# Token halves of a seven-product FFN in equal chunks, operand sums on VectorE, staged fetch for the output stage

## The chip, the cores and the metric

One NeuronCore of a Trainium2 chip runs the whole program. The metric is device time of one execution in microseconds (us), as the median of the runs shown; lower is better. The profile is one execution of the same program, taken by the hardware profiler, with times from the span's start.

## What is computed

The reference is one inference step of a two-layer backbone over 128 prompt tokens and 1024 latent tokens (1152 in all, width 1024). Layer 0 mixes tokens by retention and pooling, layer 1 by attention. Each layer ends in a SwiGLU feed-forward block (FFN), which is where the change lies. Cut to that:

```python
D_MODEL = 1024
D_FF = -(-8 * D_MODEL // (3 * 256)) * 256          # 2816

def swiglu(h, w_in, w_out):
    a, b = jnp.split(h @ w_in, 2, axis=-1)
    return (jax.nn.silu(a) * b) @ w_out

for i in range(DEPTH):                             # 2 layers
    ...                                            # mixer, residual
    fs = swiglu(rmsnorm(xs, norm_gain[i, 2]) * (1.0 + sc2s) + sh2s, w_ffn_in[i], w_ffn_out[i])
    xs = xs + g2s * rmsnorm(fs, norm_gain[i, 3])
```

Prompt tokens (xp) go the same way with their own shift, scale and gate.

## The kernel before

All matrix products keep fp32 accuracy by splitting each operand into a rounded part (hi, type fp32r) and a remainder (lo), and by summing three matmuls, hi·hi + hi·lo + lo·hi. `split` (L155 to L157) makes the pair: ScalarE (ACT) casts hi at L156, VectorE (DVE) subtracts at L157. `mm3` (L174 to L179) issues the three matmuls.

**Input half of the FFN.** The hidden width is cut in 22 tiles of 128 (f). For one f the two weight blocks (128 columns of a and 128 of b, each in two halves of the model width) form a 2x2 block matrix, and the normalised tokens form another: two halves of the model width by two halves of 576 tokens. Their product is taken in Winograd's form, with 7 block products instead of 8: P1 to P7. `PROD` (L762) says for each which weight piece or weight sum it takes ("a" or "s" and a number), which token operand (0 to 6) and which of four PSUM regions. `product` (L829) issues one: two chunks of token columns, each with 4 steps of the model width times 3 matmuls, so 24 matmuls; before, the chunks have 192 and 384 columns (L836). `prep` (L817) splits the weights of a product into one of three slots. `sums` (L809) makes the four weight sums of the next f on GpSimd (POOL). `after` (L847) takes a finished product out of PSUM; at P3 the tile's result is written to DRAM (L872).

**Prologue.** The token operands 2 to 6 are sums of token blocks and must be made first. `first_half` (L886) transposes and splits the first 576 tokens. `second_half(j, b)` (L898), eight calls, transposes tokens 576 to 1151 for one j of four and one of two column ranges (b=0: 192 wide, b=1: 384 wide), and makes the operands: sums t1 to t4 and a cast (ACT) and a subtraction for each operand. Three of the subtractions (L915, L927, L928) are on GpSimd, the rest on DVE. While this goes on, the PE runs products that need only the first operands: P1 and P2 of the first `NPRO` = 4 tiles, 8 products (`pro`, L772). They use two PSUM regions in turn, because the transposes take the other half of PSUM. `run` (L930) puts the order: product s, then `second_half`, then `after(s)`, then `prep(s + 3)`.

**Output half.** `output` (L999) multiplies the 22 tiles by w_ffn_out: 9 token tiles x 2 halves of the width, in chunks of f tiles given by `NCH`; each chunk's partial sum goes to the buffer O, by an ACT copy in the first chunk (L1038) and a DVE add after that (L1040). 22 x 18 x 3 = 1188 matmuls of 512 columns. `out_prep(f)` (L989) fetches tile f and its weights from DRAM (L992, L994), and splits them; it is called for the first two tiles during the last f of the input half and then for the tiles of the next chunk. All tiles are fetched into the same staging buffer XGT[4096:5248].

**What sets the order.** The text is handed to a list scheduler, which gives each engine its fixed sequence by a model of readiness: an instruction may be issued ahead of earlier text if its inputs are expected sooner. On the chip every engine then runs its sequence strictly in order, so an instruction that waits holds all behind it. In layer 0 small units of the next layer's adaLN projection (`Ada.unit`, `hook`) are woven into the FFN; their work is on DVE (L345) and PE (L326).

Of the kernel before, what the change touches and what calls it, by code (L numbers as in the profile page):

```python
# [10 lines left out]
F32 = mybir.dt.float32  # L11
# [53 lines left out]
def hybrid_step_kernel(ctx: ExitStack, tc: tile.TileContext, a: dict, outs: list):  # L65
# [699 lines left out]
    class FFN:  # L765
# [3 lines left out]

        def __init__(self, l, mid1, xs, xd, next_sub):  # L770
            self.l, self.M1, self.xs, self.xd, self.next_sub = l, mid1, xs, xd, next_sub
            pro = [(0, P1), (1, P1), (0, P2), (1, P2), (2, P1), (3, P1), (2, P2), (3, P2)]  # L772
            self.steps = pro + [(f, p) for f in range(NF)
                                for p in ((P6, P7, P5, P4, P3) if f < NPRO else (P1, P6, P7, P5, P2, P4, P3))]
            self.npro = len(pro)
            self.wi = a["w_ffn_in"][l].rearrange("(k p) f -> p k f", p=128)


        def xop(self, i, k, lo, c0, w):
            o = (2 * k + lo) * 576 + c0  # L780
            if i == 5:
                return self.M1[:, o:o + w]
            if i == 6:
                if (k, lo) == (3, 1):
                    return self.M1[:, 4608:4800] if c0 == 0 else RR[:, 26112:26496]
# [7 lines left out]

        def pieces(self, f, pro):
            if pro:
                b = (RAW[:, 0], RAW[:, 1], O[:, 6:8, 0:512], RAW[:, 0])[f]
# [12 lines left out]
        def sums(self, f):  # L809
            a11, a12, a21, a22 = self.pieces(f, False)  # L810
            s = [O[:, 4 + i, 576:1088] for i in range(4)]
            nc.gpsimd.tensor_tensor(s[0], a21, a22, op=ALU.add)
            nc.gpsimd.tensor_tensor(s[1], s[0], a11, op=ALU.subtract)
            nc.gpsimd.tensor_tensor(s[2], a11, a21, op=ALU.subtract)
            nc.gpsimd.tensor_tensor(s[3], a12, s[1], op=ALU.subtract)
# [13 lines left out]
        def product(self, s):  # L829
            f, p = self.steps[s]  # L830
            _, _, x, reg = PROD[p]
            if s < self.npro:
                reg = 1 - f % 2
            wh, wl = self.slot(s)
            first = p not in (P2, P3, P4)
            for c0, w, o in ((0, 192, 320), (192, 384, 512)):  # L836
                ps = PS[:, 1024 * reg + o:1024 * reg + o + w]
                n = 0
                for k in range(4):
                    ks = slice(128 * k, 128 * k + 128)  # L840
                    xh, xl = self.xop(x, k, 0, c0, w), self.xop(x, k, 1, c0, w)
                    for u, v in ((wh, xh), (wh, xl), (wl, xh)):
                        nc.tensor.matmul(out=ps, lhsT=u[:, ks], rhs=v, start=first and n == 0, stop=n == 11,  # L843
                                         skip_group_check=not first)
                        n += 1

        def after(self, s):  # L847
            f, p = self.steps[s]
            reg = PROD[p][3] if s >= self.npro else 1 - f % 2
            ps = PS[:, 1024 * reg + 320:1024 * reg + 896]  # L850
            u2, u3, c22, s1, sl = (XGT[:, 576 * i:576 * i + 576] for i in range(5))
            if f < NPRO:
                s1, sl = O[:, 2 * f, 0:576], O[:, 2 * f + 1, 0:576]
            g1, g2 = XGT[:, 2880:3456], XGT[:, 3456:4032]
            if p == P1:
                nc.scalar.copy(s1, ps)  # L856
# [41 lines left out]
        def second_half(self, j, b):  # L898

            ts, c0, w, p0 = (((4, 5), 0, 192, 64), ((6, 7, 8), 192, 384, 0))[b]  # L900
            if b == 0:
                bufs = [XGT[:, 4096 + 192 * i:4288 + 192 * i] if j % 2 == 0 else O[:, 4 + i // 3, 192 * (i % 3):192 * (i % 3) + 192]
                        for i in range(6)]
            else:
                bufs = [XGT[:, 384 * i:384 * i + 384] for i in ((0, 1, 2, 3, 8, 9) if j % 2 == 0 else (4, 5, 6, 7, 8, 9))]
            x12, x22, t1, t2, t3, t4 = bufs
            for n, (k, tm) in enumerate(((j, x12), (j + 4, x22))):
                ps = bank(4 + 2 * (j % 2) + n)
# [2 lines left out]
                self.evac_h(k, ps[:, p0:p0 + w], tm, ((1, 0, w),))  # L911
            op = lambda i, lo: self.xop(i, j, lo, c0, w)
            nc.vector.tensor_sub(t1, x12, op(0, 0))
            nc.vector.tensor_sub(t1, t1, op(0, 1))
# [3 lines left out]
            nc.vector.tensor_sub(t2, x22, t1)  # L918
            nc.scalar.copy(op(3, 0), t2)
            nc.vector.tensor_sub(op(2, 1), t1, op(2, 0))  # L920
            nc.vector.tensor_sub(t4, op(1, 0), t2)  # L921
            nc.vector.tensor_add(t4, t4, op(1, 1))  # L922
            nc.scalar.copy(op(5, 0), t4)
            nc.scalar.copy(op(4, 0), t3)
            nc.vector.tensor_sub(op(3, 1), t2, op(3, 0))
            nc.vector.tensor_sub(op(5, 1), t4, op(5, 0))
            nc.gpsimd.tensor_tensor(op(6, 1), x22, op(6, 0), op=ALU.subtract)  # L927
            nc.gpsimd.tensor_tensor(op(4, 1), t3, op(4, 0), op=ALU.subtract)  # L928

        def run(self):  # L930
            l = self.l
# [3 lines left out]
            for s in range(len(self.steps)):  # L935
                f, p = self.steps[s]
                self.product(s)
                if s < self.npro:
                    if s < 2:
                        next(tail, None)  # L940
                    if s < 7:
                        self.second_half((s + 1) % 4, (s + 1) // 4)
                    self.after(s)
                    if s + 3 < self.npro:
                        self.prep(s + 3)
                    if s == 0:
                        self.load(2, True, (0, 1))
                    elif s == 1:
                        self.load(3, True, (0, 1))
                        self.load(0, False, (2, 3))  # L950
                    elif s == 5:
                        self.load(0, False, (0, 1))
                    elif s == 6:
                        self.sums(0)
                        self.load(1, False, range(4))
                        self.prep(8)
                        self.prep(9)
                    elif s == 7:
                        self.prep(10)
                    continue  # L960
                self.after(s)
                self.prep(s + 3)
# [3 lines left out]
                    adaq.extend([Ada(1, 0, bufs, 2, True), Ada(1, 1, bufs, 2, True)])  # L966
                if f >= NPRO and p in (P7, P5):
                    hook()
                if (f, p) == (NF - 1, P1):
                    self.out_prep(1)  # L970
                elif (f, p) == (NF - 1, P7):
                    self.out_prep(0)
            self.output()


        def out_slot(self, f):
            M1, M2 = self.M1, mid2r["t"]
            r = lambda o, w: RR[:, o:o + w]
            one = lambda b: (b[:, 0:1152], b[:, 1152:2304], [b[:, 2304:2816], b[:, 2816:3328]], [b[:, 3328:3840], b[:, 3840:4352]])
            i = f % 7  # L980
            if i in (0, 1, 2, 3):
                return one(r((13824, 18432, 4608, 0)[i], 4352))
            if i == 4:
                return one(M1[:, 0:4352])
            if i == 5:
                return M2[:, 0:1152], M2[:, 1152:2304], [M2[:, 2304:2816], M2[:, 2816:3328]], [r(12288, 512), r(12800, 512)]
            return r(22784, 1152), r(23936, 1152), [r(25088, 512), r(25600, 512)], [r(26112, 512), r(13312, 512)]

        def out_prep(self, f):  # L989
            gh, gl, wh, wl = self.out_slot(f)  # L990
            gr = XGT[:, 4096:5248]
            nc.sync.dma_start(out=gr, in_=gg_scr[self.l][f])  # L992
            w = raw()
            nc.sync.dma_start(out=w, in_=a["w_ffn_out"][self.l, f * 128:(f + 1) * 128, :])  # L994
            split(gh, gl, gr)
            for h in range(2):
                split(wh[h], wl[h], w[:, 512 * h:512 * h + 512])

        def output(self):  # L999
            l = self.l  # L1000
            last_layer = self.next_sub is None
            if l == 0:
                nc.gpsimd.memset(XGT[:, 2048:3072], 0.0)
                adaq.append(Ada(1, 2, ada_bufs(XGT[:, 0:4096]), 4))
# [375 lines left out]
```

## Time and profile before

| | |
|---|---|
| median of 3 runs | 3034.7 us (3032.24 to 3035.81) |
| profiled execution, own time | 3034.96 us |
| its span | 3032.7 us, granted TensorE clock 0.988 |
| first input-half product, layer 0 / layer 1 | 693.76 / 2172.23 us |
| first product that needs the second token half (P6 of tile 0), layer 0 / 1 | 749.12 / 2232.31 us |
| first matmul of the output half, layer 0 / 1 | 1265.9 / 2734.29 us |

The page gives busy time by engine. PE is the matmul engine and PEld its weight load. In rows of groups the figures behind the bar are busy us, mean ns of one instruction, then idle time of its engine ahead of them and what ended it ("<-ACT O L1038": an ACT instruction of line 1038 that works on O). In timeline rows the first two numbers are start and length in us; matmuls in a row overlap, so n of them with a spacing p take (n - 1) p plus the length of one.

### The profile page before, as it was taken

The page shows a single profiled execution, that of the slowest core. Times are in us where ns is not written, and L with a number is a line of the kernel's source. Part 1 is how long each engine was busy: PE and PEld are TensorE (multiplying, and loading weights), DVE is VectorE, ACT ScalarE, POOL GpSimd, SP SyncE. Part 2 cuts the span into 40 slices and gives each one's busy share as a digit, 9 for nine tenths or more (in the row PEclk, how much of TensorE's full clock was granted, in tenths as well). Part 3 has the DMA queues.
Part 4 walks back from the last instruction along what each step waited for, and adds up shares of the span by engine and source line. Part 5 has one row for each costly group of instructions (what it writes and reads, how often), then busy time and mean ns, then how long its engine had stood idle before and what let it go on. Part 6 is the DMA issues. An engine that isn't in the chain of part 4 may idle for free. (4 is left out here: it accounts for less than half of the span.)

```text
span 3032.7 us, 44867 instructions
## 1 busy us (share of the span) xinstructions
PE 2927.0 (97%) x17979; PEld 2640.9 (87%) x17979; DVE 1763.9 (58%) x2793; ACT 1047.3 (35%) x1950; POOL 581.1 (19%) x766
## 2 busy tenths in 40 slices
PE   7999999998999999899999999999989999998998
PEld 4889998787999999777779988888789999997886
DVE  5783347438656666546775567884674444443554
ACT  5222223325222222321243367773532222233211
POOL 2010012115322222100034521111252222210000
PEclk9999999999999999999999999999989999999999
DMA  7531111412433333424331000002222222224322
GB/s 240 171 100 48 34 41 35 137 59 70 131 95 106 111 98 96 134 100 138 123 137 49 22 15 1 29 29 84 84 69 83 66 77 70 69 79 138 104 81 97
DMA packets 191945, 261.54 MB, mean 86 GB/s; under 512 B 10157, under 2 KB 137577, under 8 KB 191609
## 3 DMA queue, kind: packets, MB, share of 16 engines
q1 hardware_dynamic: 180160, 216.83, 22.9%
q0 software_dynamic: 11088, 41.47, 3.5%
q8 instruction: 141, 2.31, 0.3%
q14 instruction: 68, 0.55, 0.1%
q10 hardware_dynamic: 488, 0.38, 0.0%
HBM read 212.47 MB, written 46.17 MB: 85 GB/s over the span
## 5 line engine op out<-in xcount | busy, mean ns | idle before, releaser
L179 PE MATMUL PS<-RR 128*128 128x256 f32 (+2 forms) x6000 | 1068.5, 332 | 22.8 <-ACT O L1038 21.8
L179 PEld LDWEIGHTS PS<-RR 128*128 128x128 f32 x6000 | 910.8, 191 | 129.8 <-ACT O L1038 23.0
L843 PE MATMUL PS<-RR 128*128 128x192 f32 (+1 forms) x5324 | 797.6, 309 | 30.8 <-ACT O L856 15.3
L843 PEld LDWEIGHTS PS<-RR 128*128 128x128 f32 x5324 | 775.1, 193 | 41.8 <-ACT O L856 17.2
L156 ACT CAST RR<-O 128x512 fp32r<-128x512 f32 (+1 forms) x242 | 151.8, 627 | 566.2 <-PE PS L843 415.7
L179 PE MATMUL PS<-RR,MID2True 128*128 128x512 f32 (+1 forms) x1524 | 312.0, 343 | 0.1
L156 ACT CAST RR<-RAW 128x512 fp32r<-128x512 f32 (+1 forms) x187 | 135.7, 738 | 397.6 <-PE PS L179 152.6
L179 PEld LDWEIGHTS PS<-RR,MID2True 128*128 128x128 f32 x1524 | 238.9, 189 | 35.1 <-ACT MID1False L711 0.5
L157 DVE TENSOR_TENSOR RR<-RAW,RR 128x512 fp32r<-128x512 f32 (+1 forms) x187 | 157.9, 857 | 148.8 <-ACT RR L156 125.6
L1040 DVE TENSOR_TENSOR O<-PS,O 128x512 f32<-128x512 f32 x216 | 147.9, 688 | 159.2 <-PE PS L179 158.0
L157 DVE TENSOR_TENSOR RR<-O,RR 128x512 fp32r<-128x512 f32 (+1 forms) x242 | 173.0, 715 | 63.4 <-ACT RR L156 63.1
L184 POOL TENSOR_SCALAR SM<-SM 128x1 f32<-128x1 f32 (+1 forms) x153 | 52.8, 345 | 791.2 <-ACT PS L220 306.1
L345 DVE SCALAR_TENSOR_TENSOR O<-O,PW 128x512 f32<-128x512 f32 x224 | 161.0, 765 | 24.8 <-DMA O<-in_w_ada_dram 13.7
L843 PE MATMUL PS<-MID1True,RR 128*128 128x192 f32 (+1 forms) x1100 | 170.4, 305 | 0.0
L843 PEld LDWEIGHTS PS<-MID1True,RR 128*128 128x128 f32 x1100 | 160.4, 190 | 0.0
L843 PE MATMUL PS<-MID2True,RR 128*128 128x192 f32 (+1 forms) x968 | 158.7, 307 | 0.0
L179 PE MATMUL PS<-MID1True,RR 128*128 128x512 f32 (+1 forms) x576 | 145.2, 369 | 2.2 <-ACT XGT L1256 1.6
L843 PEld LDWEIGHTS PS<-MID2True,RR 128*128 128x128 f32 x968 | 143.7, 190 | 0.0
L1254 DVE TENSOR_REDUCE SM<-PS 128x1 f32<-128x1280 f32 x64 | 95.4, 1491 | 40.5 <-PE PS L179 40.1
L156 ACT CAST RR<-PS 128x512 fp32r<-128x512 f32 x160 | 93.6, 586 | 64.7 <-PE PS L1272 63.5
L179 PEld LDWEIGHTS PS<-MID1True,RR 128*128 128x128 f32 x576 | 92.5, 189 | 15.3 <-ACT XGT L1256 2.6
L157 DVE TENSOR_TENSOR RR<-PS,RR 128x512 fp32r<-128x512 f32 x160 | 103.9, 681 | 3.2 <-ACT RR L156 3.0
(291 smaller groups left out, 3274.4 us busy)
## 6 DMA issues: line engine op xcount, KB each, us to landing
O<-in_w_ada_dram SPq DMA_DIRECT2D x64, 512.0 KB
RAW<-in_w_ffn_in_dram SPq DMA_DIRECT2D x100, 256.0 KB
gg<-XGT POOLq DMA_DIRECT2D x44, 576.0 KB, 3.1
XGT<-gg SPq DMA_DIRECT2D x44, 576.0 KB
O<-in_w_ffn_in_dram SPq DMA_DIRECT2D x92, 256.0 KB
RAW<-in_w_ffn_out_dram SPq DMA_DIRECT2D x44, 512.0 KB
RAW<-in_w_in_even_dram SPq DMA_DIRECT2D x28, 512.0 KB
x<-XGT POOLq DMA_DIRECT2D x27, 512.0 KB, 3.0
```

The costliest lines, as they stand in the source:

```text
L156: nc.scalar.copy(hi, src)
L157: nc.vector.tensor_sub(lo, src, hi)
L179: nc.tensor.matmul(out=out, lhsT=x, rhs=y, start=(first and c == 0), stop=(last and c == n - 1))
L184: nc.gpsimd.tensor_scalar(r, ss, 1.0 / n, EPS, op0=ALU.mult, op1=ALU.add)
L345: nc.vector.scalar_tensor_tensor(self.acc[kind], b[:, k], sv, self.acc[kind], op0=ALU.mult, op1=ALU.add)
L843: nc.tensor.matmul(out=ps, lhsT=u[:, ks], rhs=v, start=first and n == 0, stop=n == 11, skip_group_check=not first)
L1040: nc.vector.tensor_add(dst, p3, dst)
L1254: nc.vector.reduce_max(nm, sp, axis=AX.X, negate=True)
```

## The change

- `product`: both chunks have 288 columns, still 24 matmuls; the PSUM offsets follow.
- `NPRO` is 5: P1 and P2 of a fifth tile join the prologue (10 products there, 5 instead of 7 products for tile 4 later). Its weights and results have places in XGT.
- `sums` and the three GpSimd subtractions of `second_half` move to DVE; within `second_half` the remainders come last.
- `run`: in the prologue `after(s - 1)` and `prep(s + 3)` come ahead of `second_half`; the sums of tile 0 come at s == 7.
- `out_prep` becomes `out_load` and `out_split`. There are three staging places (XGT with RAW, and a pool S2 opened where a token operand was). A tile is loaded three splits ahead; the splits are pinned to program order on ACT and DVE. `NCH` becomes (2, 3, 4, 3, 3, 3, 4) and the slots of the split tiles are laid out anew.

```diff
-NPRO = 4
-NCH = (2, 4, 3, 4, 2, 3, 4)
+NPRO = 5
+NCH = (2, 3, 4, 3, 3, 3, 4)
...
-            pro = [(0, P1), (1, P1), (0, P2), (1, P2), (2, P1), (3, P1), (2, P2), (3, P2)]
+            pro = [(0, P1), (1, P1), (0, P2), (1, P2), (2, P1), (3, P1), (2, P2), (3, P2), (4, P1), (4, P2)]
...
-            nc.gpsimd.tensor_tensor(s[0], a21, a22, op=ALU.add)
+            nc.vector.tensor_add(s[0], a21, a22)
...
-            for c0, w, o in ((0, 192, 320), (192, 384, 512)):
+            for c0, w, o in ((0, 288, 224), (288, 288, 512)):
...
             nc.vector.tensor_sub(t1, x12, op(0, 0))
+            nc.scalar.copy(op(6, 0), x22)
             nc.vector.tensor_sub(t1, t1, op(0, 1))
-            nc.gpsimd.tensor_tensor(t3, x22, x12, op=ALU.subtract)
-            nc.scalar.copy(op(6, 0), x22)
             nc.scalar.copy(op(2, 0), t1)
+            nc.vector.tensor_sub(t3, x22, x12)
+            nc.scalar.copy(op(4, 0), t3)
...
-            nc.gpsimd.tensor_tensor(op(6, 1), x22, op(6, 0), op=ALU.subtract)
-            nc.gpsimd.tensor_tensor(op(4, 1), t3, op(4, 0), op=ALU.subtract)
+                nc.vector.tensor_sub(lo, x22[:, a0:a1], hi)
+            for i, t in ((2, t1), (4, t3), (3, t2), (5, t4)):
+                nc.vector.tensor_sub(op(i, 1), t, op(i, 0))
...
+                    if 0 < s < self.npro - 1:
+                        self.after(s - 1)
+                    if s == 7:
+                        self.sums(0)
+                    self.prep(s + 3)
                     if s < 7:
                         self.second_half((s + 1) % 4, (s + 1) // 4)
-                    self.after(s)
-                    if s + 3 < self.npro:
-                        self.prep(s + 3)
...
+                    elif s >= self.npro - 2:
+                        self.after(s)
...
-                if (f, p) == (NF - 1, P1):
-                    self.out_prep(1)
-                elif (f, p) == (NF - 1, P7):
-                    self.out_prep(0)
+                if f == NF - 1:
+                    if p in (P1, P7, P2):
+                        self.out_load({P1: 1, P7: 0, P2: 2}[p])
+                    if p in (P6, P5):
+                        self.out_split({P6: 1, P5: 0}[p])
...
+        def out_raw(self, f):
+            if f < 3:
+                return XGT[:, 4096:5248], RAW[:, min(f, 1)]
+            S2 = self.S2
+            return ((S2[:, 0:1152], S2[:, 2304:3328]), (S2[:, 1152:2304], RAW[:, 0]), (XGT[:, 4096:5248], RAW[:, 1]))[f % 3]
...
+                tc.keep_in_program_order(nc.scalar.copy(hi, x))
+                tc.keep_in_program_order(nc.vector.tensor_sub(lo, x, hi))
...
+            self.S2 = open_mid2(F32)
+            self.out_load(3)
+            self.out_load(4)
...
-                        if todo and n % every == 0:
-                            self.out_prep(todo.pop(0))
+                        if todo and n >= start and (n - start) % every == 0:
+                            f = todo.pop(0)
+                            self.out_split(f)
+                            if f + 3 < NF:
+                                self.out_load(f + 3)
```

More of the change, by code (lines that the diff above doesn't have):

```diff
@@ L784, in xop @@
                 if (k, lo) == (3, 1):
-                    return self.M1[:, 4608:4800] if c0 == 0 else RR[:, 26112:26496]
+                    return self.M1[:, 4608 + c0:4608 + c0 + w] if c0 < 288 else RR[:, 25824 + c0:25824 + c0 + w]
                 return mid2r["t"][:, o:o + w]
@@ L795, in pieces @@
             if pro:
-                b = (RAW[:, 0], RAW[:, 1], O[:, 6:8, 0:512], RAW[:, 0])[f]
+                b = (RAW[:, 0], RAW[:, 1], O[:, 6:8, 0:512], RAW[:, 0], XGT[:, 3072:4096])[f]
                 return [b[:, 0:512], b[:, 512:1024]] if f != 2 else [b[:, 0], b[:, 1]]
@@ L811, in sums @@
             s = [O[:, 4 + i, 576:1088] for i in range(4)]
[L812 to L815 removed]
+            nc.vector.tensor_add(s[0], a21, a22)
+            nc.vector.tensor_sub(s[1], s[0], a11)
+            nc.vector.tensor_sub(s[2], a11, a21)
+            nc.vector.tensor_sub(s[3], a12, s[1])
         def prep(self, s):
@@ L849, in after @@
             reg = PROD[p][3] if s >= self.npro else 1 - f % 2
-            ps = PS[:, 1024 * reg + 320:1024 * reg + 896]
+            ps = PS[:, 1024 * reg + 224:1024 * reg + 800]
             u2, u3, c22, s1, sl = (XGT[:, 576 * i:576 * i + 576] for i in range(5))
-            if f < NPRO:
+            if f < 4:
                 s1, sl = O[:, 2 * f, 0:576], O[:, 2 * f + 1, 0:576]
+            elif f < NPRO:
+                s1, sl = XGT[:, 4096:4672], XGT[:, 4672:5248]
             g1, g2 = XGT[:, 2880:3456], XGT[:, 3456:4032]
@@ L904, in second_half @@
             else:
-                bufs = [XGT[:, 384 * i:384 * i + 384] for i in ((0, 1, 2, 3, 8, 9) if j % 2 == 0 else (4, 5, 6, 7, 8, 9))]
+                bufs = [XGT[:, 384 * i:384 * i + 384] for i in ((0, 1, 4, 5, 6, 7) if j % 2 == 0 else (2, 3, 4, 5, 6, 7))]
             x12, x22, t1, t2, t3, t4 = bufs
@@ L923, in second_half @@
             nc.scalar.copy(op(5, 0), t4)
-            nc.scalar.copy(op(4, 0), t3)
-            nc.vector.tensor_sub(op(3, 1), t2, op(3, 0))
-            nc.vector.tensor_sub(op(5, 1), t4, op(5, 0))
-            nc.gpsimd.tensor_tensor(op(6, 1), x22, op(6, 0), op=ALU.subtract)
-            nc.gpsimd.tensor_tensor(op(4, 1), t3, op(4, 0), op=ALU.subtract)
+            for a0, a1 in ((0, 96), (96, 384)) if (j, b) == (3, 1) else ((0, w),):
+                hi, lo = (self.xop(6, j, x, c0 + a0, a1 - a0) for x in range(2))
+                nc.vector.tensor_sub(lo, x22[:, a0:a1], hi)
+            for i, t in ((2, t1), (4, t3), (3, t2), (5, t4)):
+                nc.vector.tensor_sub(op(i, 1), t, op(i, 0))
         def run(self):
@@ L950, in run @@
                         self.load(0, False, (2, 3))
-                    elif s == 5:
+                        self.load(4, True, (0, 1))
+                    elif s == 4:
                         self.load(0, False, (0, 1))
                     elif s == 6:
-                        self.sums(0)
                         self.load(1, False, range(4))
[L956 to L959, printed above, removed]
+                    elif s >= self.npro - 2:
+                        self.after(s)
                     continue
@@ L978, in out_slot, with out_load, out_split @@
             r = lambda o, w: RR[:, o:o + w]
-            one = lambda b: (b[:, 0:1152], b[:, 1152:2304], [b[:, 2304:2816], b[:, 2816:3328]], [b[:, 3328:3840], b[:, 3840:4352]])
             i = f % 7
[L981 to L989, printed above, removed]
-            gh, gl, wh, wl = self.out_slot(f)
[L991 to L997, printed above, removed]
+            b = M1 if i == 4 else RR[:, (13824, 18432, 4608, 0, 0, 9216, 22784)[i]:]
+            w = [b[:, 2304 + 512 * x:2816 + 512 * x] for x in range(3)]
+            w.append(M1[:, 4352:4864] if i == 6 else b[:, 3840:4352])
+            return b[:, 0:1152], b[:, 1152:2304], w[0:2], w[2:4]
+        def out_raw(self, f):
[3 more added lines that the diff above has]
+            return ((S2[:, 0:1152], S2[:, 2304:3328]), (S2[:, 1152:2304], RAW[:, 0]), (XGT[:, 4096:5248], RAW[:, 1]))[f % 3]
+        def out_load(self, f):
+            g, w = self.out_raw(f)
+            nc.sync.dma_start(out=g, in_=gg_scr[self.l][f])
+            nc.sync.dma_start(out=w, in_=a["w_ffn_out"][self.l, f * 128:(f + 1) * 128, :])
+        def out_split(self, f):
+            g, w = self.out_raw(f)
+            gh, gl, wh, wl = self.out_slot(f)
+            for hi, lo, x in ((gh, gl, g), (wh[0], wl[0], w[:, 0:512]), (wh[1], wl[1], w[:, 512:1024])):
+                tc.keep_in_program_order(nc.scalar.copy(hi, x))
+                tc.keep_in_program_order(nc.vector.tensor_sub(lo, x, hi))
         def output(self):
@@ L1019, in output @@
                 todo = list(range(f0, f0 + NCH[ci + 1])) if ci + 1 < len(NCH) else []
-                every = 18 // len(todo) if todo else 99
+                start = 6 if ci == 0 else 3
+                every = (18 - start) // len(todo) if todo else 99
                 lastc = ci == len(NCH) - 1
@@ L1094, in hybrid_step_kernel @@
     F.run()
+    M2 = open_mid2(F32R)
+    mid2r["t"] = M2
     rope = XG[:, 0:2048].rearrange("p (t x) -> p t x", t=8)
```

1 line of the change is left out of this document (removed).

## The prediction

> **What bounds the kernel now.** I read the page first, then busy time by stage, then the spacing of matmuls by width, then the prologue and the entry of the output half instruction by instruction.
>
> ```profile
> span 3032.7 us, 44867 instructions
> PE 2927.0 (97%) x17979; PEld 2640.9 (87%) x17979; DVE 1763.9 (58%) x2793; ACT 1047.3 (35%) x1950; POOL 581.1 (19%) x766
> ```
>
> PE is busy nearly always, so time comes out of the change only where PE works faster or where it stands. The stages (layer 0's prologue, rest of its input half, start of its output half; the same three of layer 1; then the rest of its output half):
>
> ```profile
> core 0: us, PE busy (x) PEld busy (x) DVE busy (x) ACT busy (x) POOL busy (x), PEclk, DMA share, GB/s
> 693.76:749.12 55.36, 41.61 (x253) 39.58 (x251) 50.44 (x73) 33.04 (x75) 32.57 (x34) 0.88 0.19 57
> 749.12:1265.90 516.78, 516.62 (x3522) 502.28 (x3522) 321.40 (x429) 142.98 (x231) 126.30 (x107) 1.00 0.34 106
> 1265.90:1308.54 42.64, 30.07 (x113) 23.89 (x114) 22.72 (x32) 20.46 (x34) 1.50 (x2) 0.84 0.59 193
> 2172.23:2232.31 60.08, 41.56 (x259) 38.19 (x258) 55.47 (x90) 37.62 (x83) 35.25 (x37) 0.91 0.23 71
> 2232.31:2734.29 501.98, 501.98 (x3483) 501.87 (x3483) 233.16 (x305) 131.85 (x215) 121.42 (x104) 0.99 0.24 76
> 2734.29:2771.93 37.64, 28.41 (x114) 22.97 (x114) 13.09 (x18) 19.45 (x32) 0.53 (x1) 0.86 0.56 190
> 2771.93:2975.00 203.07, 203.07 (x885) 166.04 (x884) 97.86 (x135) 32.46 (x43) 0.00 (x0) 1.00 0.25 80
> ```
>
> Three different limits show. In the long stretches PE never stands, and only its own rate counts. In the prologues DVE is the fullest engine (55.47 of 60.08 us) and PE stands for 18.5 us. At the start of the output half nothing is full, the granted clock is 0.86, and PE waits for something else.
>
> **Chunks of 288 columns.** Layer 1 after its prologue runs 154 - 8 = 146 products in 501.98 us: 3.438 us each. What a matmul of each width takes is read from runs of one width:
>
> ```profile
> 426.20 23.88 PE L179 MATMUL PS<-RR 128*128 128x256 f32 x197
> 1013.93 1.48 PE L843 MATMUL PS<-RR 128*128 128x192 f32 x12
> ```
>
> ```profile
> L179 PE MATMUL PS<-RR 128*128 128x256 f32 x3216 | 424.2, 288 | 0.4 <-DVE RR L157 0.4
> L843 PE MATMUL PS<-RR 128*128 128x192 f32 x2640 | 334.9, 276 | 27.6 <-ACT O L856 15.3 <-ACT O L864 12.2
> ```
>
> At 256 columns the spacing is (23.88 - 0.29)/196 = 0.1204 us, at 192 (1.48 - 0.28)/11 = 0.109; the length of the last one, from the two group rows, is taken off. The 384-column spacing follows from the product, (3.438 - 12 x 0.109)/12 = 0.1775. So 64 columns more cost 0.011 us between 192 and 256, but 0.029 for each 64 between 256 and 384: the narrow chunk sits on a floor near 0.11 us that doesn't depend on its columns, and 288 columns lie beyond it. Between 256 and 384, 288 gives 0.1204 + 0.25 x 0.0571 = 0.1347; drawn from 256 to the 512-column rate of the last stage (203.07/885 = 0.2295) it is 0.1340. I take 0.1342, nearer to the second, which rests on two measured rates: a product costs 24 x 0.1342 = 3.221 us, 0.217 less. After a prologue of ten products 144 are left in each layer: 288 x 0.217 = 62 us gained. Upper end: 288 columns at the price of 256, 288 x (3.438 - 24 x 0.1204) = 158, which the slope on both sides excludes; lower end: the straight line from 192 to 384, 0.143, nothing gained.
>
> [...]
>
> **Two products more in each prologue.** They leave the stretch where PE is the limit, 2 x 2 x 3.44 = 13.8 us. What hides them is the 18.5 us that PE stands there; with that cover gone they would cost 4 x 3.22 = 12.9. P1 and P2 of the fifth tile share one PSUM region, so each of the two waits for the copy before it, about 0.65 us; that lies in the same cover.
>
> **The prologue itself.** Who holds PE, in the last full step of layer 1:
>
> ```profile
> 2225.05 4.92 PE L843 MATMUL PS<-RR 128*128 128x192 f32 x21 [5.06 <-ACT O L864]
> 2224.35 0.64 ACT L864 ACTIVATE O<-PS 128x576 f32<-128x576 f32 x1
> 2223.42 0.51 ACT L923 CAST MID1True<-XGT 128x384 fp32r<-128x384 f32 x1 [3.17 <-DVE XGT L922]
> ```
>
> PE waits for a PSUM region, ACT would free it but is queued behind a cast, the cast behind DVE. DVE's instructions there, from groups over this stage:
>
> ```profile
> L921 DVE TENSOR_TENSOR XGT<-RR,XGT 128x384 f32<-128x384 f32 x4 | 5.0, 1252 | 0.1
> L920 DVE TENSOR_TENSOR RR<-XGT,RR 128x384 fp32r<-128x384 f32 x4 | 4.9, 1218 | 0.0
> L918 DVE TENSOR_TENSOR XGT<-XGT 128x384 f32<-128x384 f32 x4 | 4.7, 1184 | 0.4
> L922 DVE TENSOR_TENSOR XGT<-XGT,RR 128x384 f32<-128x384 f32 x4 | 4.3, 1079 | 0.0
> L913 DVE TENSOR_TENSOR XGT<-XGT,RR 128x384 f32<-128x384 f32 x4 | 3.9, 964 | 1.4 <-ACT XGT L883 1.4
> L914 DVE TENSOR_TENSOR XGT<-XGT,RR 128x384 f32<-128x384 f32 x4 | 3.6, 902 | 0.1
> L925 DVE TENSOR_TENSOR RR<-XGT,RR 128x384 fp32r<-128x384 f32 x4 | 2.2, 545 | 0.0
> L925 DVE TENSOR_TENSOR RR<-XGT,RR 128x192 fp32r<-128x192 f32 x2 | 1.5, 749 | 0.0
> L925 DVE TENSOR_TENSOR RR<-O,RR 128x192 fp32r<-128x192 f32 x2 | 0.7, 346 | 0.0
> L928 POOL TENSOR_TENSOR RR<-XGT,RR 128x384 fp32r<-128x384 f32 x4 | 5.3, 1322 | 0.0
> ```
>
> The same subtraction of the same size takes 0.55 us or double, the long ones while GpSimd works beside it (L928, 1.32 us). With GpSimd's part gone the six slow groups fall from 26.4 us to 24 x 0.55 = 13.2, and at 192 columns I count two hits of 0.40 for each of four pieces, 3.2 (an estimate from the two L925 rows). DVE loses 16.4 us and receives, up to the first P6: 12 subtractions at 0.55, 12 at 0.35, one more for a split range, the four sums of tile 0 at 0.685 (below) and two more weight splits at 0.685: 6.6 + 4.2 + 0.3 + 2.7 + 1.4 = 15.2. So DVE's load stays, 1 us less. It idled 4.6 us in this stage; copies and splits now stand ahead of the operand work in ACT's and DVE's queues, so I let half of that go. P6 of tile 0 comes 3.5 us earlier in each layer: 7 us. Ends for both layers: 12 gained (all idle goes) to 16 lost (the sums and ACT's casts come one behind the other, 8 in each).
>
> **Sums on DVE in the long stretch.** Groups of layer 1 (first four) and layer 0 (last):
>
> ```profile
> L157 DVE TENSOR_TENSOR RR<-O,RR 128x512 fp32r<-128x512 f32 x90 | 61.6, 685 | 31.1 <-ACT RR L156 31.1
> L871 DVE TENSOR_TENSOR XGT<-XGT 128x576 f32<-128x576 f32 x17 | 31.1, 1828 | 2.6 <-ACT XGT L870 2.6
> L867 DVE TENSOR_TENSOR XGT<-XGT 128x576 f32<-128x576 f32 x16 | 12.0, 752 | 0.0
> L814 POOL TENSOR_TENSOR O<-O 128x512 f32<-128x512 f32 x9 | 11.6, 1288 | 80.9 <-DVE RR L157 80.9
> L345 DVE SCALAR_TENSOR_TENSOR O<-O,PW 128x512 f32<-128x512 f32 x112 | 81.9, 788 | 7.6 <-DMA O<-in_w_ada_dram 5.6 <-ACT O L343 1.5
> ```
>
> Four sums at 0.685 add 2.74 us of DVE per tile, the multiply at L871 gives back 1.08 since nothing on GpSimd is beside it. Layer 0 is the fuller one: 321.4 + 22 x 1.66 = 358 us of DVE in about 479 us (516.8 less 144 x 0.217 and two products), 75%. A weight split is due two products after its slot is free, 6.4 us; in front of it lie at most an eviction (0.76), a split (0.69), the sums (2.74) and in layer 0 four adaLN instructions (3.15), 7.3 us, but not all at once on every tile. I count zero; 1 us for each of 17 tiles of layer 0, 17 us, is the end.
>
> **Entry of the output half.** At the 0.2295 us of the undisturbed stage 114 matmuls take 26.2 us; they took 42.64 and 37.64, so 27.8 us are lost. By what:
>
> ```profile
> 2738.27 1.16 ACT L156 CAST MID1True<-XGT 128x1152 fp32r<-128x1152 f32 x1 [3.57 <-DMA XGT<-gg]
> 2744.56 1.15 ACT L156 CAST MID2True<-XGT 128x1152 fp32r<-128x1152 f32 x1 [4.09 <-DMA XGT<-gg]
> 2748.58 1.54 ACT L1038 COPY O<-PS 128x512 f32<-128x512 f32 x3
> 2749.20 23.14 PE L179 MATMUL PS<-RR 128*128 128x512 f32 x90 [9.23 <-ACT O L1038]
> 1282.19 9.21 PE L179 MATMUL PS<-RR 128*128 128x512 f32 x30 [10.52 <-ACT O L1038]
> 1291.56 1.33 ACT L343 ACTIVATE XGT<-XGT,PW 128x512 f32<-128x512 f32 x2 [5.33 <-DMA gg<-XGT]
> 1293.41 15.53 PE L179 MATMUL PS<-RR 128*128 128x512 f32 x60 [2.01 <-ACT O L1038]
> ```
>
> Splits of tiles that nobody needs yet were issued ahead and hold ACT for one fetch after the other through a single staging place; the copies that free PSUM are queued behind them. The pinned splits come at the 7th, 11th and 15th of 18 groups of the first chunk, each group 6 x 0.2295 = 1.4 us long. Their data is then asked for at least 5 us ahead, and ACT's waits for a fetch in these rows are 3.6 to 4.1 us. Late next is the ACT instruction L343 in layer 0, which the change leaves unpinned and which waits for the tile's own write: I leave 3 us there. Gain 25; ends 28 and 5. The chunks hold the same 1188 matmuls, and at the seam to layer 1 the new slots overlap the next layer's operands only behind their last use: nothing.
>
> **Sum.** From the profiled execution's 3035.0 (span 3032.7 and 2.3 around it, 0.3 over the median): 62 + 13.8 + 7 + 25 = 107.8 off, 2927.
>
> **Rivals.** (1) Spacing is linear in columns from 192 up, so equal chunks are worth what unequal ones are: 62 goes, 46 stays, 2989. Against it are the 192- and 256-column rows; for it, that no 288 is in the trace. [...] (2) The waits move rather than go: the prologue's DVE chain, longer in instructions, reaches P6 5 us later in each layer, and the output entry keeps half its loss (three of the early fetches still share XGT): 2927 + 17 + 13 = 2957. For it speaks DVE's 92% in the prologue. (3) Slower: the weight splits are held behind the sums on DVE. Its place is each turn from one tile to the next, its price what DVE's queue there exceeds 6.4 us by. From 9 us on (2.5 us lost x 44 tiles) it eats the whole gain; with the sums fully exposed it costs 44 x 2.74 = 121, 3048. Against it are the 52 to 75% load and that splits find DVE idle now (31.1 us idle ahead of L157, ended by ACT). (4) The output half's order doesn't come out as the text has it and that part stays: 2952.
>
> **Chances.** Forecast 0.70, (2) 0.13, (4) 0.06, (1) 0.06, (3) 0.03, no net change 0.02. The range 2903 to 2965 reaches from the better ends of prologue and spacing to beyond rival 2 and leaves out (1), (3) and some misses below, under 2 in 10. A difference of 0.2%, 6 us, is about what a measurement of this kernel can tell from none: faster 0.95, same 0.02, slower 0.03.
>
> **What would show it.** Rows of L843 with 288 columns and products 3.22 us apart; prologues with ten products, DVE over 90% busy, no 1.2 us subtractions, P6 of tile 0 after 52 to 57 us; L871 at 0.75; no gap over 1 us at the first output chunk in layer 1. A spacing of 0.142, PE rows ended by L157 at each tile, or an ACT cast that waits for XGT<-gg while PE stands would prove me wrong.

## The result and the profile after

After the change the kernel takes 2903.6 us (median of 4 runs, 2901.96 to 2904.19), before 3034.3 us on the same chip (4 runs, 3032.24 to 3035.81): ratio 0.957, 95% interval 0.955 to 0.959. That is 130.7 us less where 107.8 were forecast, 0.6 us inside the lower edge of the range.

The page of the kernel after, its head and the largest group of the products:

```profile
span 2902.4 us, 44728 instructions
PE 2835.7 (98%) x17979; PEld 2554.2 (88%) x17979; DVE 1796.5 (62%) x3019; ACT 1044.0 (36%) x1950; POOL 299.8 (10%) x542
L843 PE MATMUL PS<-RR 128*128 128x288 f32 x5324 | 734.2, 297 | 12.9 <-ACT RR L156 7.0
```

PE issues as many matmuls as before, is busy 91 us less and stands 39 us less; GpSimd has half its work. A comparison by stage needs one correction to the tables ahead of the prediction: their mark "P6 of tile 0" lies near the end of P6. Before, P6 starts at 741.87 and 2225.05 us, and 749.12 and 2232.31 are the start of the last two of its 24 matmuls, which wait for a remainder (L925). After, P6 starts at 738.12 and 2156.51 us. So the stages are cut here behind P6 of tile 0, where the second product of tile 0 starts. Busy time by stage, before:

```profile
core 0: us, PE busy (x) PEld busy (x) DVE busy (x) ACT busy (x) POOL busy (x), PEclk, DMA share, GB/s
693.76:749.58 55.82, 42.07 (x256) 40.03 (x255) 50.84 (x74) 33.50 (x76) 32.57 (x34) 0.88 0.19 57
749.58:1265.90 516.32, 516.17 (x3521) 501.82 (x3520) 320.99 (x429) 142.52 (x230) 126.30 (x107) 1.00 0.34 106
2172.23:2233.12 60.89, 42.37 (x262) 39.00 (x261) 56.22 (x92) 38.43 (x84) 35.25 (x37) 0.91 0.23 70
2233.12:2734.29 501.17, 501.17 (x3482) 501.06 (x3481) 232.40 (x304) 131.04 (x213) 121.42 (x104) 0.99 0.24 76
```

and after, with the first 114 matmuls of each output half as third and sixth row:

```profile
694.27:744.11 49.84, 43.55 (x303) 41.73 (x301) 45.94 (x109) 35.87 (x80) 4.23 (x5) 0.93 0.27 77
744.11:1215.99 471.88, 471.88 (x3474) 458.77 (x3473) 334.98 (x504) 136.40 (x218) 13.33 (x24) 1.00 0.37 114
1215.99:1242.64 26.65, 25.95 (x116) 21.14 (x114) 15.33 (x21) 17.23 (x29) 1.51 (x2) 1.00 0.76 244
2109.21:2161.68 52.47, 45.86 (x310) 42.84 (x308) 50.98 (x126) 40.05 (x88) 5.26 (x8) 0.93 0.30 91
2161.68:2616.43 454.75, 454.75 (x3434) 454.75 (x3433) 259.04 (x380) 124.83 (x202) 11.27 (x21) 1.00 0.26 81
2616.43:2642.09 25.66, 25.66 (x116) 21.22 (x114) 9.20 (x11) 17.20 (x29) 0.53 (x1) 1.00 0.77 268
```

| stage, both layers | before | after | difference |
|---|---|---|---|
| prologue to the end of P6 of tile 0 (9, now 11 products) | 116.7 | 102.3 | -14.4 |
| rest of the input half (145, now 143 products) | 1017.5 | 926.6 | -90.9 |
| first 114 matmuls of the output half | 80.3 | 52.3 | -28.0 |
| all else | 1818.2 | 1821.2 | +3.0 |
| span | 3032.7 | 2902.4 | -130.3 |

All else includes 2.5 us lost at the seam between the layers (last section). The spacing of matmuls and the wait of P6 after, in rows of the timeline of PE, layer 1:

```profile
2149.17 4.36 PE L843 MATMUL PS<-RR 128*128 128x288 f32 x20 [1.32 <-DVE RR L157]
2156.51 8.78 PE L843 MATMUL PS<-RR 128*128 128x288 f32 x50 [2.98 <-ACT RR L156]
2238.01 16.07 PE L843 MATMUL PS<-RR 128*128 128x288 f32 x120
```

The last row gives (16.07 - 0.30)/119 = 0.1325 us for 288 columns, so 3.18 us a product.

### The profile page after: what moved, and what is told of

Its sections match the earlier page's. It is cut to its first block, busy times and chain, and to the rows that moved or that the text cites. A ratio compares the mean times of both kernels' runs of the same rounds, so it can differ in the third digit from the quotient of the medians.

```text
span 2902.4 us, 44728 instructions
## 1 busy us (share of the span) xinstructions
PE 2835.7 (98%) x17979; PEld 2554.2 (88%) x17979; DVE 1796.5 (62%) x3019; ACT 1044.0 (36%) x1950; POOL 299.8 (10%) x542
## 5 line engine op out<-in xcount | busy, mean ns | idle before, releaser
L179 PE MATMUL PS<-RR 128*128 128x256 f32 (+2 forms) x6270 | 1134.9, 333 | 1.3 <-ACT O L1050 0.7
L843 PE MATMUL PS<-RR 128*128 128x288 f32 x5324 | 734.2, 297 | 12.9 <-ACT RR L156 7.0
L156 ACT CAST RR<-O 128x512 fp32r<-128x512 f32 (+1 forms) x242 | 151.8, 628 | 535.1 <-PE PS L843 468.7
L179 PE MATMUL PS<-RR,MID2True 128*128 128x256 f32 (+1 forms) x1416 | 269.2, 338 | 0.2 <-ACT RR L156 0.2
L179 PEld LDWEIGHTS PS<-RR,MID2True 128*128 128x128 f32 x1416 | 218.2, 189 | 30.5 <-ACT RR L156 0.8
L157 DVE TENSOR_TENSOR RR<-RAW,RR 128x512 fp32r<-128x512 f32 (+1 forms) x119 | 110.2, 932 | 101.8 <-ACT RR L156 78.7
L156 ACT CAST RR<-RAW 128x512 fp32r<-128x512 f32 (+1 forms) x119 | 95.4, 808 | 207.4 <-PE PS L843 92.4
L179 PE MATMUL PS<-MID1True,RR 128*128 128x512 f32 (+1 forms) x630 | 166.7, 372 | 2.2 <-ACT XGT L1273 1.7
L843 PE MATMUL PS<-MID1True,RR 128*128 128x288 f32 x1100 | 159.9, 295 | 0.0
L843 PE MATMUL PS<-MID2True,RR 128*128 128x288 f32 x968 | 147.0, 295 | 0.0
L184 POOL TENSOR_SCALAR SM<-SM 128x1 f32<-128x1 f32 (+1 forms) x153 | 56.6, 370 | 793.0 <-ACT PS L220 304.8
L874 POOL DMA_DIRECT2D gg<-XGT x44 | 23.6, 537 | 961.5 <-DVE XGT L873 961.5
L156 ACT CAST RR<-PS 128x512 fp32r<-128x512 f32 x160 | 93.7, 587 | 64.6 <-PE PS L1289 63.5
```

The lines of the kernel that those rows point to most:

```text
L156: nc.scalar.copy(hi, src)
L157: nc.vector.tensor_sub(lo, src, hi)
L179: nc.tensor.matmul(out=out, lhsT=x, rhs=y, start=(first and c == 0), stop=(last and c == n - 1))
L184: nc.gpsimd.tensor_scalar(r, ss, 1.0 / n, EPS, op0=ALU.mult, op1=ALU.add)
L874: nc.gpsimd.dma_start(out=gg_scr[self.l][f], in_=XGT[:, 2880:4032])
```

## The experiments

Each figure below is a median; the kernel before took 3032.2 to 3034.2 us beside them. As it differs by 2 us from one set of runs to the next, a difference of 2 or 3 us between two kernels below says little.

### The chunks alone

```diff
-            for c0, w, o in ((0, 192, 320), (192, 384, 512)):
+            for c0, w, o in ((0, 288, 224), (288, 288, 512)):
```

> The kernel before with nothing changed but the two chunks of a product: 288 and 288 columns in place of 192 and 384. Theory A (a matmul costs its columns plus an adder, and not less than about 0.109 us, so 192 columns cost 0.109, 288 cost 0.1325 and 384 cost 0.1745): a product falls from 3.43 to 3.18 us, 292 products behind the two prologues give 74 us, the prologues give nothing because VectorE sets their end: 2960 us, between 2952 and 2968. Rival L (spacing linear in columns, the gain of the change came from elsewhere): 3030 to 3036 us, a product at 3.43 us.

It took 2933.4 us, ratio 0.967 (0.965 to 0.969): 101 us less, where 74 were expected. By stage:

```profile
696.02:749.39 53.37, 37.22 (x255) 35.78 (x254) 49.94 (x75) 33.88 (x76) 33.47 (x35) 0.87 0.21 60
749.39:1227.61 478.22, 478.22 (x3522) 465.11 (x3521) 327.33 (x432) 143.10 (x229) 139.83 (x108) 1.00 0.37 115
1227.61:1259.18 31.57, 27.57 (x116) 22.30 (x114) 20.18 (x28) 19.83 (x32) 1.50 (x2) 0.95 0.72 240
2123.18:2183.22 60.04, 41.69 (x261) 37.36 (x260) 55.43 (x92) 38.45 (x84) 36.73 (x39) 0.89 0.23 71
2183.22:2644.33 461.11, 461.11 (x3483) 461.11 (x3481) 234.09 (x308) 131.65 (x213) 120.62 (x104) 1.00 0.26 83
2644.33:2670.69 26.36, 26.02 (x116) 21.05 (x114) 10.37 (x13) 17.27 (x29) 0.53 (x1) 1.00 0.70 243
```

The long stretches give 516.3 + 501.2 - 478.2 - 461.1 = 78.2 us, so theory A stands and rival L falls; the prologues give 3.3. The surprise is the output entry: 22.3 us went, though this kernel has the old output stage.

### The output stage alone, its order alone, its staging alone

The second kernel is the one before with the whole new output stage. Of the other two, one adds to the kernel before only the pins:

```diff
-            split(gh, gl, gr)
...
+                tc.keep_in_program_order(nc.scalar.copy(hi, x))
+                tc.keep_in_program_order(nc.vector.tensor_sub(lo, x, hi))
```

and one takes only the pins from the kernel after:

```diff
-                tc.keep_in_program_order(nc.scalar.copy(hi, x))
-                tc.keep_in_program_order(nc.vector.tensor_sub(lo, x, hi))
+                nc.scalar.copy(hi, x)
+                nc.vector.tensor_sub(lo, x, hi)
```

> The kernel before with the new output stage alone (loads three tiles ahead through staging, splits kept in program order, chunks of 2,3,4,3,3,3,4 tiles). Theory A: the first 114 matmuls of each output half take 26 us in place of 42.6 and 37.6, 28 us less, and nothing else moves: 3006 us, between 3002 and 3011. Rival O4 (the order of the output half comes out only with the shorter products ahead of it): 3018 us or more, with gaps of over 3 us left at its entry.

> The kernel before with nothing changed but keep_in_program_order on the splits of the output stage; one staging place, loads and chunks of tiles stay. Theory Q: the copies stand ahead of the splits now, and the entries fall from 42.6 and 37.6 us to 31 and 27 or less: 3010 to 3018 us. Rival S: pinned splits that wait for the one staging place hold the copies behind them just as long: 3028 to 3036 us.

> The kernel after without keep_in_program_order on the splits of the output stage; the loads stay three tiles ahead through staging. Theory Q (what cost 28 us was the place of the splits in ScalarE's queue, ahead of the copies that free PSUM): the splits move ahead again, and with shorter waits for data 5 to 20 us are lost at the two entries: 2909 to 2924 us. Rival S (the fetch through one staging place was the cost; with staging the order doesn't matter): 2902 to 2907 us.

The output stage alone took 3007.7 us (ratio 0.992, 0.990 to 0.993), the entries 27.7 and 25.6 us: as theory A had it. The pins alone took 3011.0 us (0.993, 0.992 to 0.995), the entries 27.4 and 27.0: theory Q, one staging place or not. The kernel after without pins took 2903.0 us (0.957, 0.956 to 0.959), the entries 25.7 twice: here the number of rival S came out, but the queue shows why. ScalarE's queue at the entry of layer 1's output half, with the chunks alone (L156 casts a split, L1040 is the copy that frees PSUM):

```profile
2644.85 1.16 ACT L156 CAST RR<-XGT 128x1152 fp32r<-128x1152 f32 x1 [1.62 <-DMA XGT<-gg]
...
2647.18 0.58 ACT L1040 COPY O<-PS 128x512 f32<-128x512 f32 x1
...
2651.01 1.16 ACT L156 CAST MID1True<-XGT 128x1152 fp32r<-128x1152 f32 x1 [0.23 <-DMA XGT<-gg]
```

with the pins alone (L996 the split, L1038 the copy):

```profile
2721.96 0.59 ACT L1038 COPY O<-PS 128x512 f32<-128x512 f32 x1
2722.45 1.16 ACT L996 CAST RR<-XGT 128x1152 fp32r<-128x1152 f32 x1
...
2727.40 0.59 ACT L1038 COPY O<-PS 128x512 f32<-128x512 f32 x1 [0.77 <-PE PS L179]
2731.13 1.16 ACT L996 CAST RR<-XGT 128x1152 fp32r<-128x1152 f32 x1 [3.14 <-DMA XGT<-gg]
```

and after without pins (L1004 the split, L1050 the copy):

```profile
2614.06 1.16 ACT L1004 CAST RR<-XGT 128x1152 fp32r<-128x1152 f32 x1 [0.39 <-DMA XGT<-gg]
2615.65 0.59 ACT L1050 COPY O<-PS 128x512 f32<-128x512 f32 x1 [0.44 <-PE PS L179]
...
2618.87 1.16 ACT L1004 CAST RR<-MID2False 128x1152 fp32r<-128x1152 f32 x1
2619.92 0.59 ACT L1050 COPY O<-PS 128x512 f32<-128x512 f32 x1
```

In the kernel before three splits in a row, each with a wait of 3.6 to 4.1 us for its fetch in layer 1, stood ahead of the first copy. In all three here copies stand between the splits; in the last, the splits find their data there. With pins alone a wait of 3.14 us is still in the queue, but copies stand ahead of it, and PE waits 1.05 us for the copies behind it, where it waited 9.23 before. So the order in ScalarE's queue was the cost. The list scheduler draws that order up anew when anything in its model moves, the width of a product included: that the new chunks mended 22 us of it was, by the queue shown, its choice and not a property of the chunks. The three cures don't add up.

### The work that went from GpSimd to VectorE

First the sums and three subtractions back on GpSimd, then the three subtractions alone:

```diff
-            nc.vector.tensor_sub(t3, x22, x12)
+            nc.gpsimd.tensor_tensor(t3, x22, x12, op=ALU.subtract)
...
-                nc.vector.tensor_sub(lo, x22[:, a0:a1], hi)
+                nc.gpsimd.tensor_tensor(lo, x22[:, a0:a1], hi, op=ALU.subtract)
```

> The kernel after with the four operand sums of a tile and the three subtractions of second_half (t3 and the remainders of operands 4 and 6) put back on GpSimd; order, chunks, five prologue tiles and output stage stay new. Theory C (GpSimd beside VectorE doubles VectorE's instructions, and VectorE's queue sets the prologue's end): the prologues go from 43.9 and 47.3 us back to 55 to 60, 20 to 28 us slower in all: 2924 to 2932 us. Rival O (the prologue became short because after() and prep() now stand ahead of second_half): under 8 us slower, 2904 to 2912 us. Rival Z (what moves to VectorE costs it as much as the contention did, the ledger of the prediction): within 4 us of 2904.

> The kernel after with the three subtractions of second_half (t3, the remainders of operands 4 and 6) back on GpSimd and the sums left on VectorE; with both back the kernel took 25 us more than after. Theory C (contention in the prologues is nearly all of those 25 us, the sums in the long stretch nothing): 2921 to 2929 us, VectorE's 384-column subtractions in the prologue again over 0.9 us in part. Rival S (half of it comes from the sums): 2910 to 2918 us.

Both back: 2929.6 us (0.966, 0.964 to 0.967), 26 us slower than after. The three alone: 2920.1 us (0.963, 0.962 to 0.965), 16.5 slower, between its two theories: the sums hold 9.5 us. The prologues with both back (two rows), then with the three alone:

```profile
694.96:755.00 60.04, 46.19 (x303) 44.58 (x302) 50.54 (x77) 36.49 (x80) 34.49 (x36) 0.89 0.21 62
2122.41:2187.32 64.91, 47.33 (x310) 44.20 (x308) 55.25 (x94) 40.75 (x88) 37.57 (x39) 0.92 0.24 74
```

```profile
694.31:750.46 56.15, 46.15 (x304) 44.80 (x301) 50.70 (x84) 36.20 (x80) 27.19 (x30) 0.88 0.23 66
2114.92:2177.24 62.32, 49.38 (x309) 46.75 (x308) 55.28 (x101) 40.58 (x88) 29.59 (x33) 0.86 0.25 77
```

Against 49.84 and 52.47 that is 22.6 and 16.2 us: most of the loss lies in the prologues, so theory C stands and O and Z fall. VectorE is busy longer with fewer instructions (94 in 55.25 us, after 126 in 50.98). One subtraction of second_half, in groups over layer 1's prologue, after and then with the three on GpSimd:

```profile
L917 DVE TENSOR_TENSOR XGT<-XGT,RR 128x384 f32<-128x384 f32 x4 | 2.2, 555 | 0.0
```

```profile
L917 DVE TENSOR_TENSOR XGT<-XGT,RR 128x384 f32<-128x384 f32 x4 | 3.8, 941 | 0.0
```

and one of the four with the three on GpSimd, beside a GpSimd instruction:

```profile
2149.08 1.34 POOL L919 TENSOR_TENSOR XGT<-XGT 128x384 f32<-128x384 f32 x1 [2.90 <-ACT XGT L885]
2149.46 1.37 DVE L917 TENSOR_TENSOR XGT<-XGT,RR 128x384 f32<-128x384 f32 x1
```

The two of the four that start while GpSimd is in an instruction last 1.30 and 1.37 us and end 0.41 us behind it; the other two last 0.55, as after. That is the contention itself. Not all of the 22.6 and 16.2 us need be its doing: ScalarE's casts now also wait for the subtraction t3 on GpSimd (L919 there), 4.1 us in layer 1's prologue with the three alone, and the runs don't part the two.

### The order of the prologue, and four tiles instead of five

```diff
-                    if 0 < s < self.npro - 1:
-                        self.after(s - 1)
...
+                    if s < 7:
+                        self.second_half((s + 1) % 4, (s + 1) // 4)
+                    self.after(s)
```

> The kernel after with the prologue's order put back: second_half, then after(s), then prep. All else is new. Theory C (VectorE's amount of work sets the prologue): 0 to 4 us slower, 2904 to 2908 us. Rival O (the order made the prologue short): 8 to 20 us slower, 2912 to 2924 us, with the prologues near 50 to 55 us.

It took 2906.6 us (0.958, 0.957 to 0.960), 3 slower, its profiled execution 2904.3: rival O falls. P6 of tile 0 starts 1.8 and 2.3 us later in it but ends as early (49.0 and 53.0 us into the prologue). The other edit sets `NPRO` to 4, with the sums of tile 0 and the preps behind them as before:

> The kernel after with four tiles in the prologue in place of five (the sums of tile 0 and the first two operand splits behind it where the kernel before has them). Theory M (two products per layer are hidden in a prologue whose length VectorE sets): 4 products of 3.18 us come back, 12.7, less what VectorE no longer does for the fifth tile: 2914 to 2919 us. Rival T (VectorE is full in the prologue already, so the fifth tile's splits lengthen it by as much as they hide): 2902 to 2908 us. Rival W (the fifth tile hides other waits as well): 2922 us or more.

It took 2915.3 us (0.961, 0.960 to 0.963), 11.7 slower: theory M. Its prologues, with nine products to the end of P6, take 48.13 and 51.35 us, 1.7 and 1.1 less than with eleven, so four products of 3.18 us lie in cover for 2.8 us.

### Other widths

Three chunks of 192 columns, then 224 and 352:

```diff
-            for c0, w, o in ((0, 288, 224), (288, 288, 512)):
+            for c0, w, o in ((0, 192, 128), (192, 192, 320), (384, 192, 512)):
```

```diff
-            for c0, w, o in ((0, 288, 224), (288, 288, 512)):
+            for c0, w, o in ((0, 224, 288), (224, 352, 512)):
```

With three chunks the kernel computes other values than the reference, and no run here shows why; number and shape of the instructions are as said.

> The kernel after with a product's 576 columns in three chunks of 192 in place of two of 288: 36 matmuls for 24. Theory A (floor of about 0.109 us for a matmul and its weight load): a product takes 36 x 0.109 = 3.92 us, 0.74 more, 288 times 214 us, and up to 10 in the prologues: 3115 to 3130 us. Rival F (no floor: a fixed adder for each matmul; from 256 and 288 columns, 0.1204 and 0.1325, the adder is 0.0137 us and 192 columns would cost 0.094): a product takes 3.37 us, 0.19 more: 2958 us. Rival L (time goes by columns alone): 2904 us.

> The kernel after with chunks of 224 and 352 columns in place of 288 and 288. Theory A (floor 0.109 us; above it columns at 0.000417 us plus 0.013): 224 columns cost 0.109, 352 cost 0.160, a product 12 x 0.269 = 3.23 us, 0.045 more, 288 times 13 us: 2912 to 2918 us. Rival F (no floor, adder alone, equal for any pair): 2904 us, within 3. Rival B (spacing bends again between 288 and 384 columns, where 384 cost 0.1745): 3.28 us or more a product: 2930 us.

Three chunks took 3173.8 us (1.046, 1.044 to 1.049). The spacing in a run of 180:

```profile
2408.19 20.26 PE L843 MATMUL PS<-RR 128*128 128x192 f32 x180
```

(20.26 - 0.28)/179 = 0.1116 us: the floor stands, and rivals F (0.094) and L fall. The time is 44 us above A's range, 27 of them since the floor is 0.1116 and not 0.109. A product takes 4.02 us, 286 x 0.84 = 240 of the 270 us lost; 22 more are in the prologues (60.0 and 64.6 us).

The pair of 224 and 352 took 2951.3 us (0.973, 0.972 to 0.975), 48 slower, where A gave 13. Its second prologue and long stretch:

```profile
2133.29:2192.38 59.09, 46.18 (x310) 43.27 (x308) 52.03 (x126) 40.50 (x88) 3.46 (x8) 0.94 0.27 83
2192.38:2661.45 469.07, 469.07 (x3435) 469.07 (x3434) 259.12 (x380) 124.81 (x202) 11.23 (x21) 1.00 0.25 79
```

and eleven of its narrow matmuls in that stretch:

```profile
2300.87 1.39 PE L843 MATMUL PS<-RR 128*128 128x224 f32 x11
```

(1.39 - 0.27)/10 = 0.112 us: 224 columns cost what 192 do. 469.07/143 is 3.28 us a product, rival B's number: with the floor at 0.109 to 0.112 a matmul of 352 columns takes 0.162 to 0.164, more than columns beyond 288 at A's price give. No run shows that price or the adders of A and of rival F, which takes the same slope: they were assumed. The spacings shown give (0.1325 - 0.1204)/32 = 0.00038 us a column from 256 to 288 and (0.2295 - 0.1204)/256 = 0.00043 from 256 to 512; a line through 256 and 288 alone comes to 0.096 at 192, which the 0.1116 refutes as it does 0.094. The 352 columns account for 29 of the 48 us; B's time, 2930 us, is missed too. Another 13 lie in the prologues (56.6 and 59.1 us): the same work on VectorE, which now idles 7 us in the second, in another order of the scheduler's. Which instruction holds it there stays open.

### The sums of tile 0 earlier

After, P6 of tile 0 waits 3 to 4 us for a split behind the sums. In the timeline, ScalarE:

```profile
2155.84 1.82 ACT L156 CAST RR<-O 128x512 fp32r<-128x512 f32 x3 [1.23 <-DVE O L812]
```

and VectorE, second_half's last instruction and the sums:

```profile
2152.38 0.56 DVE L930 TENSOR_TENSOR RR<-XGT,RR 128x384 fp32r<-128x384 f32 x1
2152.85 0.56 DVE L924 TENSOR_TENSOR XGT<-XGT,RR 128x384 f32<-128x384 f32 x1
...
2154.65 0.56 DVE L930 TENSOR_TENSOR MID1True<-XGT,MID1True 128x384 fp32r<-128x384 f32 x1 [0.31 <-ACT MID1True L925]
2155.13 0.68 DVE L812 TENSOR_TENSOR O<-RAW 128x512 f32<-128x512 f32 x1
2155.73 0.68 DVE L814 TENSOR_TENSOR O<-RAW 128x512 f32<-128x512 f32 x1
```

Two kernels move them. The first takes all four ahead, the second three and the split:

```diff
-                    if s == 7:
+                    if s == 6:
                         self.sums(0)
```

```diff
-                    if s == 7:
-                        self.sums(0)
-                    self.prep(s + 3)
+                    if s in (6, 7):
+                        self.sums(0, (s - 6,))
+                    if s != 7:
+                        self.prep(s + 3)
+                    if s == 6:
+                        self.prep(10)
```

Both also bring remainders forward. In the first the fourth sum overwrites token columns that the last transposes read, in the second the early split takes the weight slot of the eighth product before that product has run: one token operand, or one product, has other values.

> The kernel after with the sums of tile 0 a step earlier (ahead of the last second_half) and the remainders of operands 3, 4, 2, 5 ahead of that of operand 6. Theory P (P6 of tile 0 waits 3 to 4 us for an ACT split queued behind those sums, and the wait costs 2 us more in the first product after it, which runs at half the pace): 5 to 10 us faster, 2894 to 2899 us. Rival V (VectorE's amount of work up to P6 sets the end, its order doesn't): 2901 to 2906 us.

> The kernel after with the first three sums of tile 0 and the split for its P6 ahead of the last second_half, the fourth sum where it was, and the remainders of operands 4, 3 and 2 ahead of the subtractions for operand 5. The sums lie in token columns that the transposes of second_half read, the fourth in those that the last one reads; so three can go ahead and the fourth can't. Theory P (P6 waits for its split behind the sums, 3 to 4 us in each prologue, and its first product runs 0.7 to 2.8 us longer after the wait): 6 to 12 us faster than after, 2892 to 2898 us. Rival V (VectorE's work up to P6 is the same sum in any order): 2900 to 2905 us.

The first took 2900.6 us (0.956, 0.955 to 0.958), the second 2905.4 (0.958, 0.957 to 0.960). Who holds PE in the first, then in the second:

```profile
2147.90 0.90 PE L912 MATMUL PS<-CT,O 128*128 128x128 f32 x3 [3.59 <-DVE O L815]
```

```profile
2141.59 1.33 PE L845 MATMUL PS<-RR 128*128 128x288 f32 x4 [2.51 <-ACT O L868]
2152.44 9.36 PE L845 MATMUL PS<-RR 128*128 128x288 f32 x48 [2.54 <-ACT RR L156]
2162.37 3.85 PE L845 MATMUL PS<-RR 128*128 128x288 f32 x27 [0.58 <-ACT RR L156]
```

In the first the wait stands ahead of the transposes instead, and P6 starts 47.26 us into layer 1's prologue; in the kernel after it is 47.30. It ends 1.3 us earlier there, and 1.2 in layer 0, as its 24 matmuls then take some 3.9 and 4.0 us, where they took 5.17 and 5.99. In the second P6 waits only 0.6 us (last row), but the eighth and ninth products wait 2.5 us each, and P6 starts 52.05 us in. The gains of theory P didn't come: 3 us in the first, none in the second. V misses both numbers by less than half a microsecond, but neither kernel is a clean trial, since each adds a wait of its own. Whether P6 can come sooner stays open.

## Why the prediction was right, and where its sizes were off

**What bounds each stage** was right: PE's rate in the long stretches, VectorE in the prologue, a queue at the entry.

**Chunks.** The mechanism, a floor near 0.11 us under the narrow chunk, is shown by the 180 matmuls at 0.1116 and by the chunks alone. The term was mis-sized: 0.1342 was taken for 288 columns, drawn from 256 to 512 in a straight line; it is 0.1325. 286 products x (3.438 - 3.181) = 73.5 us, not 62. The 3.438 itself came out by luck: the 501.98 us hold 145 products and two matmuls, not 146 products, but the first product in them takes 6.19 us, 2.8 more than the others, and the two errors cancel. The measured widths bend: 256 to 288 columns add 0.012 us, 288 to 352 some 0.030. The linear spacing of rival 1, by which equal chunks bring nothing, is out by 78 us in the long stretches.

**Two products more in each prologue** were forecast at 13.8 and cost 11.7 us when undone.

**The prologue itself** is the step that failed in its ledger: "DVE loses 16.4 us and receives ... 15.2. So DVE's load stays, 1 us less". The prediction's mark is where VectorE has made the last remainder that P6 takes. After, all remainders are made ahead of the start of P6, and layer 1's prologue up to there is:

```profile
2109.21:2156.51 47.30, 40.77 (x285) 38.08 (x283) 46.26 (x119) 38.90 (x87) 5.26 (x8) 0.96 0.28 85
```

VectorE's busy time fell from 55.47 us to 46.26. The sum took each instruction by its duration, but undisturbed neighbours start closer than that: 2152.38 and 2152.85 in the rows above, 0.47 us apart with 0.56 each. Counted so, the six slow groups fall from 26.4 to 24 x 0.47 = 11.3, not 13.2. What moved in costs 10.1, not 15.2: 24 subtractions at 0.47 and, by 192 columns, 0.27, and two sums at 0.60; the other two sums and the two more splits come behind the start of P6. With the 3.2 of the narrow pieces that is 8.2 us less, of 9.2 measured. To the end of P6 14.4 us went in both layers where 7 were forecast. That the work on GpSimd was the cause is shown by the 22.6 us that its return costs there, the contention in it by the single instructions above; the order of the text is worth 3 at most.

**Sums in the long stretch** cost nothing, as taken: with sums and subtractions on GpSimd the stretches behind P6 take 473.7 and 454.8 us, after 471.9 and 454.8. The multiply of L871 (L873 after) fell from 1.83 to 0.75 us, as forecast.

**Output entry.** 28.0 for 25. The place, splits ahead of copies, was right. But the prediction gave the gain to the pinned order with its early fetch; the order alone brings 21 us, staging without it is as good, and the chunks had most of it by themselves. In layer 0 3 us were left for the adaLN instruction; its first 114 matmuls take 1.0 us longer than layer 1's, 0.7 of it one wait for a copy.

**Sum.** 73.5 + 13.8 + 14.4 + 28.0 = 129.7, and 0.6 net from the rest (a slow product of 2.8 us and some tenths gone from the long stretches, 3.0 lost elsewhere), against 62 + 13.8 + 7 + 25. No term came out smaller than forecast, and three of four were larger, so the range held by 0.6 us only. Rival 1 falls to the chunks alone, rival 4 to the entries of the kernel after. Of rivals 2 and 3 nothing showed: PE is busy 454.75 of 454.75 us behind layer 1's prologue. A wait did move, that of P6, but inside a prologue that got shorter.

## What to carry to other kernels

Price a queue by the starts of neighbours, not by their durations (here 0.47 us apart and 0.56 long), and count two engines that slow each other once at the slow and once at the free price (here 0.94 and 0.56 us on the mean for one subtraction). Where a scheduler orders a queue, read the order out of the trace before crediting a gain to an edit, and try the edits one by one: three of them each cured the same wait. Equal chunks beat unequal ones here, where the narrow one sat on the floor of a matmul, 0.109 to 0.112 us at 192 and 224 columns.

## What the runs showed that was not expected

PE's pace after a wait differs for waits of one length. After the 2.98 us ahead of P6, and at the seam between the layers, the granted clock over the next 5 to 8 us was, in the kernel after:

```profile
2156.51:2161.68 5.17, 5.09 (x25) 4.76 (x25) 4.72 (x8) 1.16 (x2) 0.00 (x0) 0.67 0.52 152
1523.53:1531.90 8.37, 8.37 (x51) 8.27 (x50) 4.70 (x11) 1.78 (x6) 0.90 (x2) 0.68 0.77 259
```

and before, at the same seam:

```profile
1589.35:1595.15 5.80, 5.80 (x48) 5.80 (x49) 3.89 (x9) 1.19 (x5) 1.14 (x2) 1.00 0.92 308
```

The wait ahead of the seam's matmuls was 2.74 us after and 2.75 before; 47 matmuls then took 8.35 us after, 46 took 5.77 before. That is the 2.5 us lost there, and no instruction of the change stands in it. With the old order of the prologue P6 started later, with 0.81 us as the last wait ahead of it, and took 3.4 us, not 5.2: that is how it ended as early. What makes the clock fall at one seam and not at the other, no run here shows.
